# Both feature tiles of a pair in one run of gate matmuls: recurrent gates of a hybrid streaming block

## The chip, the cores and the metric

One core of a Trainium2 chip. TensorE (PE) multiplies, its weight loads (PEld) run beside it; VectorE (DVE), ScalarE (ACT) and GpSimd (POOL) do elementwise work; SyncE (SP) issues most of the transfers. The metric is the device time of one execution in microseconds, as the median of several. Less is better.

## The reference, cut to what matters

One layer over 512 frames of width 1024. The part that the change touches is the recurrent branch: a projection, a causal convolution, and two block-diagonal gates of 64x64 blocks that drive a linear recurrence.

```python
xn = rmsnorm(h, norm_mix_g[l])
u = jnp.einsum('bsd,de->bse', xn, w_in[l])
q, k, v, xr, gr, ga, gb = jnp.split(u, splits, axis=-1)
...
xc = causal_depthwise_conv(xr, conv_w[l], conv_b[l])
hr = rg_lru(xc, w_rg_r[l], b_rg_r[l], w_rg_i[l], b_rg_i[l], rg_lambda[l])
yb = (hr * jax.nn.gelu(gr)) @ w_rnn_out[l]

def rg_lru(x, w_r, b_r, w_i, b_i, lam):
    xb = x.reshape(B, S, N_RG_BLOCKS, RG_BLOCK)
    r = jax.nn.sigmoid(jnp.einsum('bsnd,nde->bsne', xb, w_r).reshape(B, S, D) + b_r)
    i = jax.nn.sigmoid(jnp.einsum('bsnd,nde->bsne', xb, w_i).reshape(B, S, D) + b_i)
    log_a = -RG_C * r * jax.nn.softplus(-lam)
    a = jnp.exp(log_a)
    bx = jnp.sqrt(-jnp.expm1(2.0 * log_a)) * (i * x)
    ...
```

## The kernel before

Features lie on the 128 partitions and frames on the free axis, so the 1024 features of a branch are eight tiles `j` of 128 x 512 (`S` is 512). All operands of TensorE are split into a high and a low part, and a product is three matmuls: high by high, high by low, low by high (`mm3`, lines 76 to 78). A projection of one tile, such as `po_xr`, is eight such triples, 24 matmuls of 512 columns.

The recurrent branch runs over pairs of tiles, `j` and `j + 1`, in the loop `for j in range(0, KT, 2)` at the end of the printed code: four pairs. For each pair come the two projections `po_xr` with their convolutions (`rnn_conv`), the two projections `po_gr` with their GeLU (`rnn_gelu`), the gates (`gates_of`, `rnn_gates`), and two projections `po_gb` for the merge gate (`gate`). In the first pair the `po_xr` and `po_gr` projections are done in two halves of 256 frames.

`rnn_conv` makes `xc` from `po_xr` with one activation (line 469) and three taps on VectorE (line 471). ScalarE copies it to the high part of `xch` (line 473), and POOL subtracts to get the low part (line 474). `rnn_gates` then multiplies `xch` with `wrg`, whose upper and lower 64 rows hold the blocks of one feature block each: six matmuls on half of the rows (line 492), alternating between the lower and the upper half (`e` is 1, then 0), each half into a bank of its own of the tile `rg`. Two matmuls on different halves of the rows can be in TensorE at the same time. Four activations of 64 partitions read the banks (lines 496 and 497), further ones and VectorE, POOL follow, and when both tiles of a pair have come so far, one square root over both (line 533) and the scans end it (`rnn_scan`). In `rnn_gelu`, the last VectorE step (line 483) is the last to read `po_gr`.

PSUM has eight banks here: four of the tag `mm`, in which most projections lie, two of the tag `t`, and the two of `rg`. A bank is written again when the engine that reads it last is through.

What sets the order: the program is written as above, and a scheduler places each instruction on its engine's queue by a simulated timeline, so the six matmuls of a run may come later than they are written. Inside the block `tc.manual_schedule` TensorE's instructions stay together in program order. Each queue is worked off in order; a waiting instruction holds what is behind it. POOL also computes the softplus of the recurrence's parameter (`sp_p`, lines 426 to 434) in many small steps, VectorE and ScalarE convert the weights (`whl`, lines 82 and 83), and VectorE forms differences of weight blocks that go back to memory (the spills, line 582).

Of the kernel before, what the change touches and what calls it, by code (L numbers as in the profile page):

```python
# [8 lines left out]
F32 = mybir.dt.float32  # L9
F32R = mybir.dt.float32r  # L10
AF = mybir.ActivationFunctionType
# [3 lines left out]
P = 128  # L15
D = 1024
S = 512
# [3 lines left out]
HD = 64  # L21
# [15 lines left out]
def block_kernel(ctx: ExitStack, tc: tile.TileContext, x, norm_mix_g, w_in, b_merge, rel_table,  # L37
# [3 lines left out]
    pe, dve, act, pool, sp = nc.tensor, nc.vector, nc.scalar, nc.gpsimd, nc.sync  # L41
# [23 lines left out]
    rgp = rg_stack.enter_context(tc.tile_pool(name="rg", bufs=1, space=PSUM, reuse_waits="tile"))  # L65
# [5 lines left out]
    def mm_tile(name, tag="mm"):  # L71
        return ps.tile([P, S], F32, tag=tag, bufs=4 if tag == "mm" else 2, name=name)
# [315 lines left out]
    hb = cp.tile([P, 40], F32, name="hb")  # L388
# [58 lines left out]
    wrg = rw2.tile([P, 2, 8, P], F32R, bufs=1, name="wrg")  # L447
# [8 lines left out]
    def halves(e):  # L456
        own, other = slice(e * HD, e * HD + HD), slice(HD - e * HD, 2 * HD - e * HD)
        return own, other
# [4 lines left out]
    def rnn_conv(j, po_xr):  # L463

        def tap(w):
            return vc[:, V_CW + 8 * w + j:V_CW + 8 * w + j + 1]

        xc = rw.tile([P, S], F32, tag="xc", name=f"xc{j}")
        act.activation(xc[:], po_xr[:], AF.Identity, bias=vc[:, V_CB + j:V_CB + j + 1], scale=tap(3))
        for d in range(1, 4):  # L470
            dve.scalar_tensor_tensor(xc[:, d:S], po_xr[:, 0:S - d], tap(3 - d), xc[:, d:S], ALU.mult, ALU.add)  # L471
        xch = rw2.tile([P, 2, S], F32R, tag="xch", name=f"xch{j}")
        act.activation(xch[:, 0], xc[:], AF.Copy)
        pool.tensor_sub(xch[:, 1], xc[:], f(xch[:, 0]))
        return xc, xch

    def rnn_gelu(j, po_gr):

        g = rw.tile([P, S], F32, tag="g", name=f"g{j}")
        act.activation(g[:], po_gr[:], AF.Square, scale=(GELU_C * GELU_A) ** 0.5)  # L480
        dve.scalar_tensor_tensor(g[:], g[:], GELU_C, po_gr[:], ALU.add, ALU.mult)
        act.activation(g[:], g[:], AF.Tanh)
        dve.scalar_tensor_tensor(g[:], g[:], 1.0, po_gr[:], ALU.add, ALU.mult)
        return g

    def rnn_gates(j, xc, xch, g):
        pos = rgp.tile([P, 2, S], F32, tag="rg", bufs=1, name=f"rg{j}")
        with tc.manual_schedule(engines={mybir.EngineType.PE}):
            for i, (w, x_) in enumerate(((0, 1), (0, 0), (1, 0))):
                for e in (1, 0):  # L490
                    rows = slice(e * HD, e * HD + HD)
                    pe.matmul(pos[:, e], wrg[rows, w, j], xch[rows, x_], start=i == 0, stop=i == 2)
        tr, ti = (rw.tile([P, S], F32, tag=f"gt{n}", bufs=(2, 3)[n], name=f"gt{j}_{n}") for n in range(2))
        for e in range(2):
            own, other = halves(e)
            act.activation(tr[own, :], pos[own, e], AF.Tanh, bias=hb[own, j:j + 1], scale=0.5)
            act.activation(ti[own, :], pos[other, e], AF.Tanh, bias=hb[other, 32 + j:33 + j], scale=0.5)
        if j % 2 == 0:
            u_pairs.append(rw.tile([P, 2, S], F32, tag="u", bufs=2, name=f"u{j}"))
        u = u_pairs[-1][:, j % 2]  # L500
        act.activation(u, tr[:], AF.Tanh, bias=sp2[:, j:j + 1], scale=sp2[:, j:j + 1])
        act.activation(tr[:], tr[:], AF.Exp, bias=spm4[:, j:j + 1], scale=spm4[:, j:j + 1])

        dve.scalar_tensor_tensor(u, tr[:], 1.0, u, ALU.add, ALU.mult)
        a = rw.tile([P, S], F32, tag="a", bufs=3, name=f"a{j}")
        pool.tensor_scalar(a[:], u, -1.0, 1.0, ALU.mult, ALU.add)

        dve.scalar_tensor_tensor(u, u, 2.0, u, ALU.subtract, ALU.mult)
        dve.scalar_tensor_tensor(ti[:], ti[:], 1.0, xc[:], ALU.add, ALU.mult)
        return j, u, a, ti, g  # L510
# [4 lines left out]
    def rnn_scan(j, u, a, ti, g):  # L515
        dve.scalar_tensor_tensor(ti[:], ti[:], 0.5, u, ALU.mult, ALU.mult)
        dve.tensor_tensor_scan(u, a[:], ti[:], 0.0, ALU.mult, ALU.add)
        dve.scalar_tensor_tensor(u, u, 0.5, g[:], ALU.mult, ALU.mult)
        if j % 2 == 0:
            rnn_pairs.append(big(j // 2, [P, 2, 2, S], F32R, f"rnn{j}"))  # L520
        o = rnn_pairs[-1][:, j % 2]
        act.activation(o[:, 0], u, AF.Copy)
        pool.tensor_sub(o[:, 1], u, f(o[:, 0]))
        return o
# [2 lines left out]
    rnn_pairs = []  # L527
    held = []

    def gates_of(j):  # L530
        held.append(rnn_gates(j, *conv.pop(j)))
        if len(held) == 2:
            act.activation(u_pairs[-1][:], u_pairs[-1][:], AF.Sqrt, scale=-1.0)
            while held:
                rnn.append(rnn_scan(*held.pop(0)))

    def tile_of(name, c, tag="mm", ahead=1):

        whl = weights(name, ahead)
        if (name, c) in first:  # L540
            po = first[name, c]
            project(po, whl, c, xnT, 256, S)
        else:
            po = mm_tile(f"po_{name}_{c}", tag)
            project(po, whl, c, xnT)
        return po
# [5 lines left out]
    def gate(w, j):  # L552
        po = tile_of(f"g{'ab'[w]}{j - j % 2}", j % 2)
        act.activation((ta, zB)[w][j], po[:], AF.Tanh, bias=hb[:, 16 + 8 * w + j:17 + 8 * w + j], scale=0.5)
# [37 lines left out]
    def spill_of(w, u, pl, tag, bufs):  # L592
        name, unit, to = {id(w_v): ("v", units_v, sums_v), id(w_o): ("o", units_o, sums_o)}.get(id(w), ("f", units, sums_d))
        r = [pl.tile([P, 2, S], F32, tag=tag, bufs=bufs, name=f"spill{name}{u}_{n}")[:] for n in range(4)]
        return spill(w, unit[u], to[u], r, w is w_o)
# [21 lines left out]
    def at_once(steps):  # L617
        for _ in steps:
            pass
# [3 lines left out]
    conv = {}  # L623
    for j in range(0, KT, 2):
        if j >= 4:
            at_once(spill_of(w_v, j // 2 - 2, early, "spill", 4))
        for c in range(2):
            conv[j + c] = rnn_conv(j + c, tile_of(f"xr{j}", c, ahead=2))
        for c in range(2):
            po = tile_of(f"gr{j}", c, "mm" if j == 0 else "t")  # L630
            conv[j + c] += (rnn_gelu(j + c, po),)
            gates_of(j + c)
        for c in range(2):
            gate(1, j + c)

# [714 lines left out]
    for j in range(4, FT, 2):  # L1350
# [5 lines left out]
        g, u = (sc.tile([P, 4, 256], F32, tag=f"c{w}", name=f"c_{w}{j}") for w in "gu")  # L1356
# [142 lines left out]
    with tc.manual_schedule(engines={mybir.EngineType.PE, mybir.EngineType.DVE, mybir.EngineType.Activation}):  # L1499
# [44 lines left out]
        x, w = acts["a22", last[0]], parts_w["t4", last[0]]  # L1544
# [39 lines left out]
```

## Time and profile before

| | |
|---|---|
| median of 3 runs | 852.59 us (852.57 to 852.69) |
| the profiled execution's own time | 852.42 us |
| its span | 850.5 us |
| mean granted clock of TensorE | 0.998 |
| matmuls of the gates, line 492 | 48, in 8 runs of six, from 43.3 to 145.9 us |
| activations on their banks, lines 496 and 497 | 32 of 64x512, about 0.68 us each |

The profile is of one execution, taken on the chip. A row of the timeline gives the start and the duration in us, the engine, the line in the program, the operation, what it writes and reads, the shape, and in brackets how long the engine sat idle before it and who released it. Matmuls are pipelined, so their rows overlap: the step from one start to the next is what one costs, not the duration. Rows of stretches give the busy time of each engine, then the granted clock of TensorE as a share of full speed (PEclk), then the transfers.

### The profile page before, as it was taken

The numbers are of one execution on the slowest core, as the hardware profiler recorded it, in microseconds if no ns is written. First come the engines' busy times: TensorE is split into PE (matmuls) and PEld (weight loads), VectorE is DVE, ScalarE is ACT, GpSimd is POOL, SyncE is SP. The second block draws the span as 40 slices with busy tenths as digits, with TensorE's granted clock in tenths as the row PEclk, the third lists the DMA queues.
The fourth block names the chain that finished last, engine by engine and source line by source line (L and its number), as shares of the span: only waits on it lengthen the run. The fifth ranks groups of instructions, "written<-read, shape, count | busy, mean of one in ns | idle before, by whom it ended". The sixth has DMA issues, their size and how long they took to land.

```text
span 850.5 us, 13164 instructions
## 1 busy us (share of the span) xinstructions
PE 839.3 (99%) x4836; PEld 733.8 (86%) x4836; DVE 676.0 (79%) x1029; ACT 513.8 (60%) x878; POOL 173.3 (20%) x192
## 2 busy tenths in 40 slices
PE   8999999999999999999999999999999999999997
PEld 6977887888888888888888889999999999988885
DVE  5789767699686777665678888998999897699985
ACT  7678686723665677656564558566465565285554
POOL 2324302220022576755500040000000001000002
PEclk9999999999999999999999999999999999999999
DMA  8684332695557246645456441677547332896622
GB/s 276 190 311 168 99 99 62 204 334 193 173 161 218 79 140 221 198 137 161 149 179 241 149 149 50 198 274 257 189 159 245 117 125 91 275 320 205 198 74 100
DMA packets 117776, 152.48 MB, mean 179 GB/s; under 512 B 7632, under 2 KB 86080, under 8 KB 117712
## 3 DMA queue, kind: packets, MB, share of 16 engines
q1 hardware_dynamic: 114032, 143.98, 52.0%
q10 hardware_dynamic: 3680, 7.67, 2.9%
q8 instruction: 38, 0.62, 0.3%
q14 instruction: 26, 0.21, 0.1%
HBM read 126.42 MB, written 25.21 MB: 178 GB/s over the span
## 4 chain that ended last, share of the span: by engine, by line
PE 90%; DVE 3%; POOL 3%; ACT 2%; issue 1%; DMA 1%; ACTq 0%; SPq 0%; DVEq 0%; POOLq 0%
PE po_out L76 4%; PE po_out L77 4%; PE po_out L78 4%; PE p_fu L76 3%; PE p_fu L77 2%; PE p_fu L78 2%; PE p_fg L76 2%; PE p_fg L77 2%; PE p_fg L78 2%; POOL p L718 2%; PE po_gb L76 2%; PE po_gb L77 2%; PE po_ya L78 2%; PE po_gb L78 2%; PE po_k L76 2%; PE po_ya L76 2%
## 5 line engine op out<-in xcount | busy, mean ns | idle before, releaser
L718 POOL TENSOR_SCALAR p<-p,rl 128x128 f32<-128x128 f32 (+1 forms) x64 | 49.3, 790 | 122.3 <-DVE rl L716 122.2
L1298 POOL TENSOR_TENSOR act_lo<-act,act_hi 128x1024 fp32r<-128x1024 f32 x1 | 2.4, 2422 | 215.9 <-ACT act_hi L1297 215.9
L713 ACT ACTIVATE p<-p,m 128x128 f32<-128x128 f32 (+1 forms) x64 | 35.7, 560 | 9.7 <-DVE m L712 9.5
L83 DVE TENSOR_TENSOR pp<-pT,pp 128x384 fp32r<-128x384 f32 (+1 forms) x48 | 28.6, 599 | 16.2 <-ACT pp L82 15.9
L83 DVE TENSOR_TENSOR whl_t<-raw_t,whl_t 128x1024 fp32r<-128x1024 f32 x26 | 31.6, 1214 | 0.3 <-ACT whl_t L82 0.3
L712 DVE CUSTOM_DVE_ANT_0 p<-s,bias 128x128 f32<-128x128 f32 (+1 forms) x64 | 29.5, 483 | 0.2
L1495 POOL TENSOR_TENSOR h<-h,g_fin 128x512 f32<-128x512 f32 x4 | 5.1, 1292 | 116.6 <-ACT oj L1491 116.6
L76 PE MATMUL po_gr<-xnT,whl_gr 128*128 128x512 f32 (+1 forms) x80 | 28.2, 354 | 0.1
L82 ACT ACTIVATE whl_t<-raw_t 128x1024 fp32r<-128x1024 f32 x26 | 27.2, 1046 | 1.5 <-PE po_h L78 1.5
L77 PE MATMUL po_xr<-xnT,whl_xr 128*128 128x512 f32 (+1 forms) x80 | 27.8, 353 | 0.0
L77 PE MATMUL po_gr<-xnT,whl_gr 128*128 128x512 f32 (+1 forms) x80 | 27.6, 347 | 0.0
L78 PE MATMUL po_gr<-xnT,whl_gr 128*128 128x512 f32 (+1 forms) x80 | 27.5, 348 | 0.0
L78 PE MATMUL po_xr<-xnT,whl_xr 128*128 128x512 f32 (+1 forms) x80 | 27.3, 346 | 0.0
L76 PE MATMUL po_xr<-xnT,whl_xr 128*128 128x512 f32 (+1 forms) x80 | 26.7, 352 | 0.6 <-ACT xnT L329 0.6
L76 PE MATMUL po_ga<-xnT,whl_ga 128*128 128x512 f32 x64 | 25.3, 396 | 0.3 <-DVE oacc L753 0.3
L83 DVE TENSOR_TENSOR whl_fg_s<-s_fg,whl_fg_s 128x1024 fp32r<-128x1024 f32 x18 | 21.9, 1220 | 4.7 <-ACT whl_fg_s L82 4.7
L76 PE MATMUL po_gb<-xnT,whl_gb 128*128 128x512 f32 x64 | 25.3, 395 | 0.2 <-DVE xc L471 0.2
L77 PE MATMUL po_gb<-xnT,whl_gb 128*128 128x512 f32 x64 | 25.2, 393 | 0.0
L76 PE MATMUL po_q<-xnT,whl_qk 128*128 128x512 f32 x64 | 25.1, 393 | 0.0
L78 PE MATMUL po_ga<-xnT,whl_ga 128*128 128x512 f32 x64 | 25.0, 390 | 0.0
L78 PE MATMUL po_q<-xnT,whl_qk 128*128 128x512 f32 x64 | 25.0, 390 | 0.0
L78 PE MATMUL po_ya<-aT,whl_ya 128*128 128x512 f32 x64 | 25.0, 390 | 0.0
(523 smaller groups left out, 3340.6 us busy)
## 6 DMA issues: line engine op xcount, KB each, us to landing
raw_t<-sums SPq DMA_DIRECT2D x20, 512.0 KB, 4.4
raw_fu<-in_w_ffn_in_dram SPq DMA_DIRECT2D x18, 512.0 KB, 4.1
raw_fg<-in_w_ffn_in_dram SPq DMA_DIRECT2D x18, 512.0 KB, 3.8
raw_qk<-in_w_in_dram SPq DMA_DIRECT2D x32, 256.0 KB, 3.5
raw_b<-in_w_ffn_out_dram SPq DMA_DIRECT2D x15, 512.0 KB, 4.8
spillf<-in_w_ffn_out_dram SPq DMA_DIRECT2D x12, 512.0 KB, 6.7
sums<-spillf SPq DMA_DIRECT2D x12, 512.0 KB, 3.0
raw_xr<-in_w_in_dram SPq DMA_DIRECT2D x8, 512.0 KB, 4.7
```

The costliest lines, as they stand in the source:

```text
L76: pe.matmul(o, sh, mh, start=start, stop=False, skip_group_check=parts)
L77: pe.matmul(o, sh, ml, start=False, stop=False, skip_group_check=parts)
L78: pe.matmul(o, sl, mh, start=False, stop=stop, skip_group_check=parts)
L82: act.activation(hi, src, AF.Copy)
L83: dve.tensor_sub(lo, src, f(hi))
L712: dve.tensor_tensor_reduce(prob[qb][:], scs[qb], bias[:, S - w:S], -1.0, 3e38, ALU.add, ALU.min, nmax[:, qb:qb + 1])
L713: exp = act.activation(prob[qb][:], prob[qb][:], AF.Exp, bias=nmax[:, qb:qb + 1], scale=-1.0, accum_out=lsum[:, qb:qb + 1])
L718: pool.tensor_scalar(prob[qb][:], prob[qb][:], rl[:, qb:qb + 1], 1.0, ALU.mult, ALU.mult)
L1298: pool.tensor_sub(lo[:], o[:], f(hi[:]))
L1495: eng.tensor_mul(hs, hs, g_fin[:, cc * S + at.start:cc * S + at.stop])
```

## The change

The matmuls leave `rnn_gates`, and a new function `rnn_products` does those of both tiles of a pair in one manually ordered block of twelve, after both GeLUs are written. The even tile keeps the two banks of `rg`; the odd tile takes two `mm` banks. The activations read the bank that they are given. Arithmetic, operands and the number of instructions on TensorE stay.

```diff
-    def rnn_gates(j, xc, xch, g):
-        pos = rgp.tile([P, 2, S], F32, tag="rg", bufs=1, name=f"rg{j}")
+    def rnn_products(js):
+        banks = {}
+        for j in js:
+            if j % 2:
+                banks[j] = [mm_tile(f"rg{j}_{e}")[:] for e in range(2)]
+            else:
+                both = rgp.tile([P, 2, S], F32, tag="rg", bufs=1, name=f"rg{j}")
+                banks[j] = [both[:, e] for e in range(2)]
         with tc.manual_schedule(engines={mybir.EngineType.PE}):
-            for i, (w, x_) in enumerate(((0, 1), (0, 0), (1, 0))):
-                for e in (1, 0):
-                    rows = slice(e * HD, e * HD + HD)
-                    pe.matmul(pos[:, e], wrg[rows, w, j], xch[rows, x_], start=i == 0, stop=i == 2)
+            for j in js:
+                for i, (w, x_) in enumerate(((0, 1), (0, 0), (1, 0))):
+                    for e in (1, 0):
+                        rows = slice(e * HD, e * HD + HD)
+                        pe.matmul(banks[j][e], wrg[rows, w, j], conv[j][1][rows, x_], start=i == 0, stop=i == 2)
+        return banks
+
+    def rnn_gates(j, pos, xc, xch, g):
         tr, ti = (rw.tile([P, S], F32, tag=f"gt{n}", bufs=(2, 3)[n], name=f"gt{j}_{n}") for n in range(2))
         for e in range(2):
             own, other = halves(e)
-            act.activation(tr[own, :], pos[own, e], AF.Tanh, bias=hb[own, j:j + 1], scale=0.5)
-            act.activation(ti[own, :], pos[other, e], AF.Tanh, bias=hb[other, 32 + j:33 + j], scale=0.5)
+            act.activation(tr[own, :], pos[e][own], AF.Tanh, bias=hb[own, j:j + 1], scale=0.5)
+            act.activation(ti[own, :], pos[e][other], AF.Tanh, bias=hb[other, 32 + j:33 + j], scale=0.5)
...
-    def gates_of(j):
-        held.append(rnn_gates(j, *conv.pop(j)))
+    def gates_of(j, pos):
+        held.append(rnn_gates(j, pos, *conv.pop(j)))
...
             conv[j + c] += (rnn_gelu(j + c, po),)
-            gates_of(j + c)
+        banks = rnn_products((j, j + 1))
+        for c in range(2):
+            gates_of(j + c, banks[j + c])
```

The scheduler answers with another order. TensorE in the first pair before, from the end of the second `po_gr` (`po_gr0_1`) on; `po_gb0_0` goes on for 24 matmuls:

```order
L76 MATMUL po_gr0_1_356<-xnT_158,whl_gr0_4_328 128x256
L77 MATMUL po_gr0_1_356<-xnT_158,whl_gr0_4_328 128x256
L78 MATMUL po_gr0_1_356<-xnT_158,whl_gr0_4_328 128x256
L76 MATMUL po_gb0_0_690<-xnT_158,whl_gb0_0_491 128x512 [waits DVE_49,Activation_49]
L77 MATMUL po_gb0_0_690<-xnT_158,whl_gb0_0_491 128x512
```

and at the end of `po_gb0_0`, where tile 0's run of six (`rg0`, on `xch0`) stood:

```order
L77 MATMUL po_gb0_0_690<-xnT_158,whl_gb0_4_496 128x512
L78 MATMUL po_gb0_0_690<-xnT_158,whl_gb0_4_496 128x512
L492 MATMUL rg0_592<-xch0_528,wrg_431 128x512 [waits Pool_49]
L492 MATMUL rg0_592<-xch0_528,wrg_431 128x512
L492 MATMUL rg0_592<-xch0_528,wrg_431 128x512 [waits Activation_49]
L492 MATMUL rg0_592<-xch0_528,wrg_431 128x512 x3
L76 MATMUL po_gb0_1_716<-xnT_158,whl_gb0_0_491 128x512 [waits Activation_49]
```

Tile 1's run followed 15 matmuls into the next pair's first `po_xr`. TensorE at the same place with the change (`rg1_0` and `rg1_1` are the odd tile's two `mm` banks):

```order
L78 MATMUL po_gr0_1_356<-xnT_158,whl_gr0_4_328 128x256
L499 MATMUL rg0_621<-xch0_528,wrg_431 128x512 [waits Pool_49]
L499 MATMUL rg0_621<-xch0_528,wrg_431 128x512
L499 MATMUL rg0_621<-xch0_528,wrg_431 128x512 [waits Activation_49]
L499 MATMUL rg0_621<-xch0_528,wrg_431 128x512 x3
L499 MATMUL rg1_1_623<-xch1_560,wrg_431 128x512 [waits PE_49,Pool_49]
L499 MATMUL rg1_0_622<-xch1_560,wrg_431 128x512 [waits DVE_49,PE_49]
L499 MATMUL rg1_1_623<-xch1_560,wrg_431 128x512 [waits Activation_49]
L499 MATMUL rg1_0_622<-xch1_560,wrg_431 128x512
L499 MATMUL rg1_1_623<-xch1_560,wrg_431 128x512
L499 MATMUL rg1_0_622<-xch1_560,wrg_431 128x512
L76 MATMUL po_gb0_0_688<-xnT_158,whl_gb0_0_491 128x512 [waits DVE_49]
```

All twelve have moved ahead of both `po_gb`, and the run waits for POOL twice, for `xch0` and for `xch1`. In the three later pairs the twelve stand in the same way between the second `po_gr` and the first `po_gb`; before, a pair's first run stood in the middle of the second `po_gr` or just ahead of it, and its second run within a `po_gb`.

ScalarE around the first pair's gates before (`xch1` is tile 1's high part, `zb0` the activation on `po_gb`):

```order
L482 ACTIVATE g0_587<-g0_587 128x512 [waits DVE_49]
L482 ACTIVATE g1_640<-g1_640 128x512 [waits DVE_49]
L554 ACTIVATE zb0_438<-po_gb0_0_690,hb_385 128x512 [waits PE_49]
L496 ACTIVATE gt0_0_602<-rg0_592,hb_385 64x512 [waits PE_49]
L497 ACTIVATE gt0_1_603<-rg0_592,hb_385 64x512
L496 ACTIVATE gt0_0_602<-rg0_592,hb_385 64x512
L497 ACTIVATE gt0_1_603<-rg0_592,hb_385 64x512
L473 ACTIVATE xch1_560<-xc1_555 128x512 [waits DVE_49,Activation_49]
```

and with the change:

```order
L482 ACTIVATE g0_587<-g0_587 128x512 [waits DVE_49]
L506 ACTIVATE gt0_0_639<-rg0_621,hb_385 64x512 [waits PE_49]
L507 ACTIVATE gt0_1_640<-rg0_621,hb_385 64x512
L506 ACTIVATE gt0_0_639<-rg0_621,hb_385 64x512
L507 ACTIVATE gt0_1_640<-rg0_621,hb_385 64x512
L482 ACTIVATE g1_616<-g1_616 128x512 [waits DVE_49]
L473 ACTIVATE xch1_560<-xc1_555 128x512 [waits DVE_49,Activation_49]
```

The second GeLU step `g1` has gone behind tile 0's four gate activations, `zb0` further back; `xch1` still stands behind tile 0's gates.

## The prediction

> **What bounds the kernel now.** I read the busy times first, then the chain that ended last, then TensorE's waits.
>
> ```profile
> PE 839.3 (99%) x4836; PEld 733.8 (86%) x4836; DVE 676.0 (79%) x1029; ACT 513.8 (60%) x878; POOL 173.3 (20%) x192
> PE 90%; DVE 3%; POOL 3%; ACT 2%; issue 1%; DMA 1%; ACTq 0%; SPq 0%; DVEq 0%; POOLq 0%
> PE pT L731 <- POOL p L718: 1.3, 4, 0.3
> PE busy L278 <- DVE eps_t L284: 1.2, 1, 1.2
> L492 PE MATMUL rg<-xch,wrg x48: 386/394/497, 43.3 to 145.9; 64*128 64x512 f32 x48
> ```
>
> TensorE is busy for 99% of the span and carries 90% of the chain. In the list of waits (total us, times, longest) its longest single wait is 1.2 us, at the start. So there is no idle time later on in which a new stall could be absorbed: a microsecond that TensorE loses early is a microsecond at the end. The question is then what the change does to TensorE's own time in the four feature pairs, and whether the longer run must wait for its operands. The gate matmuls run from 43.3 to 145.9 us, so all of it lies in the first sixth of the span.
>
> **What one run of six costs.** From the timeline of TensorE, second pair (start, duration, instruction):
>
> ```profile
> 69.73 0.39 PE L78 MATMUL po_gr<-xnT,whl_gr 128*128 128x512 f32 x1
> 70.05 0.50 PE L492 MATMUL rg<-xch,wrg 64*128 64x512 f32 x2
> 70.38 0.62 PE L492 MATMUL rg<-xch,wrg 64*128 64x512 f32 x4
> 70.62 0.39 PE L492 MATMUL rg<-xch,wrg 64*128 64x512 f32 x2
> 70.94 0.50 PE L76 MATMUL po_gr<-xnT,whl_gr 128*128 128x512 f32 x1
> 73.58 0.39 PE L78 MATMUL po_gr<-xnT,whl_gr 128*128 128x512 f32 x1
> 73.81 0.39 PE L76 MATMUL po_gb<-xnT,whl_gb 128*128 128x512 f32 x1
> ```
>
> Plain matmuls of 512 columns start 0.227 us apart (73.58 to 73.81). From 69.73 to 73.81 there are 13 of those steps, 2.95 us, so the run of six cost 4.08 - 2.95 = 1.13 us. The half-row matmuls go two at a time: pairs start at 70.05, 70.38 and 70.62, so a third pair behind a second costs 0.24 us. Three pairs more in the same run would cost 3 x 0.24 = 0.72 us, and a run of twelve saves 1.13 - 0.72 = **0.41 us** against two of six. The bounds: 0.45 if the added pairs go at the plain step of 0.227, 0.24 if six more cost all the 0.89 us that lie between 70.05 and 70.94.
>
> The ideal gain is therefore 4 x 0.41 = 1.6 us. No row tells this from no change safely: 0.2% of the time, 1.7 us, is about what a measurement can separate.
>
> **The wait that it adds.** In the changed order TensorE's queue holds the first pair's twelve matmuls right behind the second `po_gr` and ahead of both `po_gb`. The six of tile 0 wait for POOL's `xch0`, the six of tile 1 for POOL's `xch1`; behind them is everything else that TensorE does. When is each there? In the order of POOL, ScalarE and VectorE up to `xch1`, only two things differ: the four gate activations of tile 0 now stand ahead of the second `L482`, and `zb` of `po_gb` has gone behind.
>
> ```profile
> 37.19 0.28 PE L78 MATMUL po_gr<-xnT,whl_gr 128*128 128x256 f32 x1
> 37.66 0.47 PE L76 MATMUL po_gb<-xnT,whl_gb 128*128 128x512 f32 x1 [0.19 <-DVE xc L471]
> 43.30 0.96 PE L492 MATMUL rg<-xch,wrg 64*128 64x512 f32 x6
> 41.51 0.23 POOL L433 TENSOR_SCALAR sp_p<-sp_p 128x8 f32<-128x8 f32 x1
> 41.70 1.30 POOL L474 TENSOR_TENSOR xch<-xc,xch 128x512 fp32r<-128x512 f32 x1
> 47.83 1.95 POOL L474 TENSOR_TENSOR xch<-xc,xch 128x512 fp32r<-128x512 f32 x1 [3.68 <-ACT xch L473]
> 46.00 0.74 DVE L471 SCALAR_TENSOR_TENSOR xc<-po_xr,vc,xc 128x509 f32<-128x509 f32 x1
> 44.30 0.68 ACT L496 ACTIVATE gt<-rg,hb 64x512 f32<-64x512 f32 x1 [0.21 <-PE rg L492]
> 47.12 0.63 ACT L473 ACTIVATE xch<-xc 128x512 fp32r<-128x512 f32 x1
> 47.65 0.80 ACT L501 ACTIVATE u<-gt,sp 128x512 f32<-128x512 f32 x1
> ```
>
> - TensorE is through with `po_gr` at 37.19 + 0.12 = 37.31. Before, it began `po_gb` at 37.66 and worked until 43.30.
> - `xch0` is ready at 41.70 + 1.30 = 43.00: it sits on POOL behind the small operations of the softplus (`sp_p`), whose order does not change. A released matmul started 0.15 us after its releaser (`xc` 37.51, `po_gb` 37.66), so the first six start at 43.15. **Idle: 43.15 - 37.31 = 5.8 us.**
> - The gate activations started 1.00 us after the run (43.30, 44.30) and the four took 2.82 us until 47.12. Now: 44.15 to 46.97. Then the second `L482`, about 0.53 us (the step from 47.12 to 47.65 for the same shape), then `xch1` on ScalarE at 47.50. `xc1` is ready at 46.74, so VectorE is not last. The step to POOL's start was 0.71 us (47.12, 47.83): 48.21. I take the same instruction's 1.95 us, since VectorE works beside it as before: ready at 50.16, second six at 50.31.
> - The first six end at 43.15 + 0.89 = 44.04. **Idle: 50.31 - 44.04 = 6.3 us.**
>
> The sum of the first pair: 5.8 + 6.3 of new idle time, less the 0.35 us that TensorE waited before `po_gb` (37.31 to 37.66), less what the idle hides of two runs' entries and exits: each run's 1.13 is 0.68 of streaming and 0.45 of the rest, of which only the last exit, about 0.35, is still paid, so 0.55. That is **+11.2 us**. With POOL's subtraction at 1.30 it is 10.6, at its longest, 3.25, it is 12.5.
>
> ```profile
> L474 POOL TENSOR_TENSOR xch<-xc,xch x8: 1285/1296/3245, 41.7 to 138.9; 128x512 fp32r<-128x512 f32 x8
> 76.42 3.25 POOL L474 TENSOR_TENSOR xch<-xc,xch 128x512 fp32r<-128x512 f32 x1 [10.75 <-issue]
> 104.99 1.28 POOL L474 TENSOR_TENSOR xch<-xc,xch 128x512 fp32r<-128x512 f32 x1 [0.68 <-POOL xch L474]
> 138.86 1.29 POOL L474 TENSOR_TENSOR xch<-xc,xch 128x512 fp32r<-128x512 f32 x1 [4.17 <-issue]
> 108.71 0.39 PE L76 MATMUL po_gb<-xnT,whl_gb 128*128 128x512 f32 x1
> 138.03 0.50 PE L76 MATMUL po_gr<-xnT,whl_gr 128*128 128x512 f32 x1
> ```
>
> The other three pairs: a run now stands behind the whole second `po_gr` instead of inside it or later, so its odd tile is wanted earlier. In the third pair `xch5` is ready at 106.27 (104.99 + 1.28) and that place is at 108.71 - 1.13 = 107.6; in the fourth `xch7` is ready at 140.15 and the place at 138.03 + 24 x 0.227 - 1.13 = 142.4. In the second `xch3` was ready at 79.67 only, and 73.81 - 1.13 = 72.7 would have been the place. But before, VectorE put the first pair's scans between the taps of `xc3`; now these are done while TensorE stands still, and the taps follow `po_xr` directly. I count `xch3` ready some 6 us after its `po_xr`, with the place 10.9 us after it (two `po_gr`). So I expect no wait in these, and a gain of 3 x 0.41 = **-1.2 us** (-0.7 to -1.35).
>
> **The clock.** Two pauses of about 6 us with 0.9 us of work between them are longer than any that TensorE has had. Its granted clock (the column PEclk of the stretches) shows what a pause does, at the end of this trace, and its first matmuls show what a restart costs:
>
> ```profile
> 843.89 0.28 PE L78 MATMUL po_rest<-whl_t,x_a 128*128 128x256 f32 x1
> 845.00:846.00 1.00, 0.00 (x0) 0.00 (x0) 0.87 (x5) 0.55 (x3) 0.00 (x0) 1.00 0.00 0
> 846.00:847.00 1.00, 0.00 (x0) 0.00 (x0) 0.58 (x2) 0.61 (x1) 0.00 (x0) 0.86 0.00 0
> 847.00:848.00 1.00, 0.00 (x0) 0.00 (x0) 0.00 (x0) 0.00 (x0) 0.00 (x0) 0.50 0.45 181
> L278 PE MATMUL busy<-idle x16: 379/634/634, 1.2 to 7.3; 128*128 128x512 bf16 x16
> ```
>
> The last matmul starts at 843.89 and the clock stands at 0.50 from about 846.72 (0.28 of that microsecond at half gives its 0.86): 2.7 us of idle time were enough. At the start, 16 matmuls of 512 columns start between 1.18 and 7.3, 0.41 us apart, where 0.227 is the later step: 15 x 0.18 = 2.7 us lost until full speed. I take that as the price of the restart at the second six (another number type, so an estimate; 0 if the clock holds, 3.4 if the slow stretch lasts a microsecond or two longer). The first six run slow too: 0.7 us more (three steps of 0.24 doubled; 0 to 0.9), which delays the gates and with them `xch1`. Together **+3.4 us**.
>
> [...]
>
> **Edits that cost nothing here.** The odd tile's gates take two of the four `mm` banks, and `po_gb` of the first pair now waits for VectorE to leave `po_gr`'s bank: `L483` did that by 45 us, TensorE comes at 51. ScalarE loads one activation table more:
>
> ```profile
> 44.27 0.68 DVE L483 SCALAR_TENSOR_TENSOR g<-g,po_gr 128x512 f32<-128x512 f32 x1
> 64.26 1.28 ACT L533 ACT_TABLE_LOAD   x1
> 51.38 1.22 DVE L83 TENSOR_TENSOR whl_gr<-raw_gr,whl_gr 128x1024 fp32r<-128x1024 f32 x1
> ```
>
> Its 1.28 us lie beside the 11 us of both `po_gb`; without that cover they would delay the next pair's weights by as much. Those are the edit to watch: `whl_gr` of the second pair, 51.38 before, now stands on VectorE behind the whole first pair up to the scans. Counted on from the gates at 51.3: eight gate and decay operations to 55.6, table and root to 59.3, scans, products and two of the spill's subtractions to about 67, the conversion to 68.2. TensorE needs it after `po_gb` and `po_xr`, 4 x 5.45 us from 51.2: 73. Five us to spare. On SP the loads of `raw_gb` and `raw_xr` have gone behind more of the spill's stores; they are for use after 84 us.
>
> **The sum.** The profiled execution took 852.42 us (span 850.5), 0.17 under the median of the three runs, 852.59. 852.42 + 11.2 - 1.2 + 3.4 = **865.8 us**.
>
> **The rivals.**
> - *The clock holds* through the pauses, or falls too late to matter: 865.8 - 3.4 = 862.4. For it: the pauses are cut by six matmuls. Against it: the drop after 2.7 us. Chance 0.12.
> - *A second stall follows*: the first pair's work on VectorE and ScalarE is bunched, and if a spill's load comes late, the second pair's `whl_gr` misses the 73 us, or its `xch3` the end of `po_gr` at 84. Both have about 5 us to spare; a slip of 8 gives 865.8 + 3 = 868.8. Chance 0.07.
> - *Not slower*: both `xch` are there when TensorE arrives. Then only the merging counts, 852.42 - 4 x 0.41 = 850.8. It would need `xch1` before 37.3; but `xc1` alone leaves VectorE at 46.74, and nothing ahead of it there has moved. That the twelve do not run as one is ruled out by the order. Chance 0.03, of which 0.01 lies within 0.2%.
>
> **The numbers.** The forecast, with the stall and the clock, has 0.78, and by its terms' bounds goes from about 863.5 to 868. The range takes in the clock's rival: 862.0 to 868.5. Faster by over 0.2%: 0.02; within: 0.01; slower: 0.97.
>
> **What would show it.** Right: TensorE idle for some 6 us before the first `rg` matmul and again before the seventh, both times with POOL's `xch` as the releaser; `po_gb` beginning at 51 to 53 us instead of 37.66; a granted clock of 0.50 there; later runs of twelve taking about 1.85 us with no wait ahead. Wrong: no pause between the sixth and seventh matmul, a pause at a later pair, or a clock of 1.00 from 37 to 60 us.

## The result and the profile after

The changed kernel takes **864.58 us** (median of 4 runs, 863.81 to 865.69); the kernel before took 852.64 us beside it (852.57 to 853.10). The ratio is 1.0141, 95% interval 1.0129 to 1.0154: slower, as forecast, by 1.2 us less than the forecast of 865.8. The profiled execution is the fastest of the four, 863.81 us.

The page of the changed kernel, its rows on the span, the busy times, the granted clock and the chain:

```profile
span 861.9 us, 13162 instructions
PE 839.6 (97%) x4836; PEld 735.8 (85%) x4836; DVE 680.7 (79%) x1029; ACT 514.8 (60%) x878; POOL 173.3 (20%) x192
PEclk9979999999999999999999999999999999999999
PE 87%; POOL 4%; DVE 3%; ACT 2%; DMA 1%; issue 1%; ACTq 0%; SPq 0%; DVEq 0%; POOLq 0%
```

TensorE works for as long as before (839.6 against 839.3 us), in a span that is 11.4 us longer, so what was added is idle time. The third slice of the clock (43 to 65 us) reads 7 tenths, where it read 9 before, and POOL's share of the chain went from 3% to 4%. The list of TensorE's waits (total us, times, longest) has one new row of more than 1 us, and the timeline shows where it lies and what the clock does to the matmuls behind it:

```profile
PE rg L499 <- POOL xch L474: 10.9, 2, 5.6
```
```profile
37.15 0.28 PE L78 MATMUL po_gr<-xnT,whl_gr 128*128 128x256 f32 x1
42.98 1.65 PE L499 MATMUL rg<-xch,wrg 64*128 64x512 f32 x6 [5.55 <-POOL xch L474]
50.03 1.72 PE L499 MATMUL rg<-xch,wrg 64*128 64x512 f32 x6 [5.39 <-POOL xch L474]
51.68 0.80 PE L76 MATMUL po_gb<-xnT,whl_gb 128*128 128x512 f32 x1
52.27 0.63 PE L77 MATMUL po_gb<-xnT,whl_gb 128*128 128x512 f32 x1
...
53.55 0.47 PE L77 MATMUL po_gb<-xnT,whl_gb 128*128 128x512 f32 x1
53.86 0.39 PE L78 MATMUL po_gb<-xnT,whl_gb 128*128 128x512 f32 x1
54.09 0.39 PE L76 MATMUL po_gb<-xnT,whl_gb 128*128 128x512 f32 x1
```

Two pauses stand where the forecast put them, before the first gate matmul and before the seventh, and `po_gb` begins at 51.68 instead of 37.66 us. Up to 53.55 the matmuls go at half speed (0.43 us from start to start), then at the usual 0.23. The stretches of the same trace (the number before the last two is the granted clock) give the moments: it falls at 40.06 and is back at 53.72.

```profile
40.00:41.00 1.00, 0.00 (x0) 0.00 (x0) 1.00 (x2) 0.15 (x1) 0.99 (x1) 0.53 0.19 54
42.00:50.00 8.00, 1.65 (x6) 0.84 (x6) 7.23 (x11) 5.22 (x8) 3.34 (x3) 0.50 0.66 238
53.00:54.00 1.00, 1.00 (x4) 0.77 (x4) 0.69 (x1) 0.95 (x3) 0.28 (x1) 0.64 0.90 195
```

The later pairs do run as one, without a wait ahead. The second pair in the timeline:

```profile
85.17 0.39 PE L78 MATMUL po_gr<-xnT,whl_gr 128*128 128x512 f32 x1
85.48 1.66 PE L499 MATMUL rg<-xch,wrg 64*128 64x512 f32 x12
87.07 0.50 PE L76 MATMUL po_gb<-xnT,whl_gb 128*128 128x512 f32 x1
```

From the last matmul ahead to the first behind are 1.90 us, where a run of six took 1.21 before (69.73 to 70.94). Six more cost 0.69 us instead of 1.13.

The account closes in this execution. `po_gb` starts 14.02 us late and its first matmuls lose another 0.9 us to the clock (51.68 to 54.09 are 2.41 us, for 0.34 + 5 x 0.23 = 1.49). Off go the two runs of six that stood later before, 2.26, and three merges of 0.44: 14.02 + 0.92 - 2.26 - 1.3 = 11.4 us, as measured (863.81 against 852.42).

### The profile page after: what moved, and what is told of

Same layout as the page of the kernel before. It is cut to its first block, busy times and chain, and to the rows that moved or that the text cites. A ratio compares the mean times of both kernels' runs of the same rounds, so it can differ in the third digit from the quotient of the medians.

```text
span 861.9 us, 13162 instructions
## 1 busy us (share of the span) xinstructions
PE 839.6 (97%) x4836; PEld 735.8 (85%) x4836; DVE 680.7 (79%) x1029; ACT 514.8 (60%) x878; POOL 173.3 (20%) x192
## 4 chain that ended last, share of the span: by engine, by line
PE 87%; POOL 4%; DVE 3%; ACT 2%; DMA 1%; issue 1%; ACTq 0%; SPq 0%; DVEq 0%; POOLq 0%
PE po_out L76 4%; PE po_out L77 4%; PE po_out L78 4%; PE p_fu L76 2%; PE p_fu L77 2%; PE p_fu L78 2%; PE p_fg L76 2%; PE p_fg L77 2%; PE p_fg L78 2%; POOL p L730 2%; PE po_gb L76 2%; PE po_gb L77 2%; PE po_gb L78 2%; PE po_ya L76 2%; PE po_ya L77 2%; PE po_ya L78 2%
## 5 line engine op out<-in xcount | busy, mean ns | idle before, releaser
L730 POOL TENSOR_SCALAR p<-p,rl 128x128 f32<-128x128 f32 (+1 forms) x64 | 47.5, 762 | 122.1 <-DVE rl L728 122.0
L76 PE MATMUL po_gb<-xnT,whl_gb 128*128 128x512 f32 x64 | 25.9, 405 | 0.0
L77 PE MATMUL po_gb<-xnT,whl_gb 128*128 128x512 f32 x64 | 25.3, 395 | 0.0
L83 DVE TENSOR_TENSOR whl_qk<-raw_qk,whl_qk 128x1024 fp32r<-128x1024 f32 x16 | 20.9, 1327 | 5.3 <-ACT whl_qk L82 5.1
L78 PE MATMUL po_gb<-xnT,whl_gb 128*128 128x512 f32 x64 | 25.1, 393 | 0.0
L76 PE MATMUL po_q<-xnT,whl_qk 128*128 128x512 f32 x64 | 25.1, 393 | 0.0
```

Source lines behind the costliest of these rows:

```text
L76: pe.matmul(o, sh, mh, start=start, stop=False, skip_group_check=parts)
L77: pe.matmul(o, sh, ml, start=False, stop=False, skip_group_check=parts)
L78: pe.matmul(o, sl, mh, start=False, stop=stop, skip_group_check=parts)
L83: dve.tensor_sub(lo, src, f(hi))
L730: pool.tensor_scalar(prob[qb][:], prob[qb][:], rl[:, qb:qb + 1], 1.0, ALU.mult, ALU.mult)
```

## The experiments

Three things were open. Why does the run stand ahead of both `po_gb` at all: because it is one run of twelve, or because of the banks? Does the merging as such save what the rows say, in a pair that does not stall? And what do the two parts of the loss, the pauses and the clock, cost each by itself?

| kernel | median us | ratio to before, on the same chip | 95% interval |
|---|---|---|---|
| the change | 864.58 | 1.0141 | 1.0129 to 1.0154 |
| e4_banks_alone | 865.98 | 1.0150 | 1.0137 to 1.0164 |
| e1_first_apart | 860.19 | 1.0083 | 1.0069 to 1.0097 |
| e2_behind_gb | 866.59 | 1.0161 | 1.0147 to 1.0175 |
| e3_kept_busy | 866.87 | 1.0159 | 1.0145 to 1.0173 |
| e3b_busy_longer | 865.22 | 1.0140 | 1.0127 to 1.0154 |
| e8_busy_low_on_dve | 862.97 | 1.0114 | 1.0097 to 1.0131 |
| e5_first_only | 865.49 | 1.0144 | 1.0130 to 1.0158 |
| e7_last_two | 852.06 | 0.9988 | 0.9979 to 0.9997 |

### The banks without the run of twelve

The kernel before, with its eight separate runs of six, but the odd tile in two `mm` banks:

```diff
-            gates_of(j + c)
+            gates_of(j + c, rnn_products((j + c,))[j + c])
```

> Runs of six for each tile again, written where they were before, with the odd tile in two mm banks: the banks without the run of twelve. If the banks decide (the odd tile takes the two banks that are free first, so both po_gb are left with banks that the second convolution and the second GeLU hold until 46 and 47 us): pauses ahead of both runs of the first pair as in the changed kernel, about 864.6 + 3 x 0.2 to 3 x 0.42 = 865.2 to 865.9 us. If the run of twelve decides: no pauses and 852.6 us.

Measured: ratio 1.0150, and the changed kernel's row among the waits:

```profile
PE rg L499 <- POOL xch L474: 11.0, 2, 5.6
```

So the banks alone bring the whole stall. In the built program the first pair's `po_xr` and `po_gr` hold all four `mm` banks. Before, `po_gb` took the bank of `po_xr0`, which the taps of `xc0` free at about 37.5 us. Now the odd tile takes that bank and the one of `po_gr0`, and `po_gb` is left with the banks of `po_xr1` and `po_gr1`, still to be read by the second convolution (its last tap ends at 46.66 us) and the second GeLU. For the scheduler `po_gb` is then the later of the two, and the gates go first. The place of the run is therefore not the harm by itself: put first, `po_gb` would have waited for the bank of `po_xr1` until about 46.7 us (an estimate from that last tap). What a run of twelve in other banks would do was not run.

### The first pair as before, three pairs merged

```diff
-            if j % 2:
+            if j % 2 and j > 1:
...
+            if j == 0:
+                gates_of(c, rnn_products((c,))[c])
-        banks = rnn_products((j, j + 1))
-        for c in range(2):
-            gates_of(j + c, banks[j + c])
+        if j:
+            banks = rnn_products((j, j + 1))
+            for c in range(2):
+                gates_of(j + c, banks[j + c])
```

> The change undone in the first pair alone: its two tiles have a run of six each in the banks of rg, as before; the three later pairs keep the run of twelve with the odd tile in mm banks. My theory (the whole loss comes from the first pair, and a run of twelve saves about 0.42 us against two of six): 852.6 - 3 x 0.42 = 851.3 us, no wait ahead of any gate matmul, clock 1.00 throughout the pairs. Rival, that a longer run saves nothing (the time between runs is only moved): 852.6 us. Rival, that the later pairs lose too by the banks they take: above 853 us.

Measured: ratio 1.0083, where 851.3 us would have been 0.9985. A clear miss, by more than 8 us: the stall has moved into the second pair. The waits and the timelines of TensorE and POOL there:

```profile
PE rg L499 <- POOL xch L474: 7.2, 2, 6.2
```
```profile
73.92 0.39 PE L78 MATMUL po_gr<-xnT,whl_gr 128*128 128x512 f32 x1
74.24 0.96 PE L499 MATMUL rg<-xch,wrg 64*128 64x512 f32 x6
81.38 1.65 PE L499 MATMUL rg<-xch,wrg 64*128 64x512 f32 x6 [6.18 <-POOL xch L474]
77.58 3.74 POOL L474 TENSOR_TENSOR xch<-xc,xch 128x512 fp32r<-128x512 f32 x1 [9.62 <-issue]
```

This is the place that the prediction weighed: `xch3` was ready only at 79.67 us before, and the run wants it at 72.7. Here it is ready at 81.32, wanted at 75.1. In the changed kernel nothing waits there, because VectorE and POOL catch up while TensorE stands in the first pair: VectorE's first scan (`u<-a,gt`) begins there at 63.56 us, before the second pair's `po_xr` are through (74.5), and here at 73.75, 10 us after them (63.3). The first stall hides the second. So merging is free in the second pair only after a stall has been paid for. There is a smaller miss as well: the other wait of the row, 1.1 us, is that of the first pair's second run at 54.75 us, since POOL's subtraction for `xch1` took 6.52 us. The two waits, the second pair's second six at half speed (0.7) and the slow start of `po_gb` (0.8), less three merges (1.3), are 7.4 us. In the profiled execution the first `po_q`, the product behind the four pairs, begins 8.0 us later than before (163.67 against 155.63), 0.4 of it from ahead of the gates (`po_gb` began at 38.02 instead of 37.66).

### The products written behind both `po_gb`

```diff
+        for c in range(2):
+            gate(1, j + c)
         banks = rnn_products((j, j + 1))
         for c in range(2):
             gates_of(j + c, banks[j + c])
-        for c in range(2):
-            gate(1, j + c)
```

> The products written behind both po_gb of their pair, so that po_gb takes its banks first. In the order the first pair then has tile 0's six between the po_gb and tile 1's six behind them; the later pairs have twelve behind the second po_gb. If the first pair's loss comes from the banks that the odd tile takes ahead of po_gb: no 5 us pauses there, po_gb begins near 37.7 us, and the merging gives 851.3 us, unless the last pair's scans, now some 10 us later, are late for po_yb; then up to 5 us more, seen as a wait of po_yb for rnn at about 165 us (851 to 857). If the loss came from having both tiles' products in one block: pauses of 5 us at 37 to 50 us and 863 us or more.

Measured: ratio 1.0161, another miss. `po_gb` takes its bank first and covers the wait for `xch0`, so the first pause is gone. But the seventh matmul still waits, 4.4 us, and a new wait of 4.2 us appears in a later stage. There TensorE waits for VectorE's `zb`, which stands at 200.58 us behind VectorE's other work, without a gap since 182.0; the wait for `rnn` that was expected there is only 0.4 us. The waits; POOL's subtraction that makes `xch1`; and VectorE's last instructions before it came to an end:

```profile
PE rg L499 <- POOL xch L474: 4.4, 1, 4.4
PE po_yb L76 <- DVE zb L894: 4.2, 1, 4.2
```
```profile
48.10 6.50 POOL L474 TENSOR_TENSOR xch<-xc,xch 128x512 fp32r<-128x512 f32 x1 [3.70 <-ACT xch L473]
...
51.65 0.69 DVE L514 SCALAR_TENSOR_TENSOR u<-gt,u 128x512 f32<-128x512 f32 x1
52.25 1.22 DVE L83 TENSOR_TENSOR whl_gr<-raw_gr,whl_gr 128x1024 fp32r<-128x1024 f32 x1
```

The subtraction of 128x512 took 1.27 us in the changed kernel and 6.50 here. It ends 1.13 us after VectorE's first gap (52.25 + 1.22 = 53.47, and 54.60). In this order VectorE's instructions follow each other without a gap from 47.64 to 53.47, and `xch1` is there at 54.60 instead of 49.98: the order that covers the first wait delays the second operand. In its twelve the scheduler put a whole `po_gb` between the first six and the second: the ordered block keeps only the order of its own instructions, and others may stand between. To that extent the description above, that they stay together, is too strong.

### TensorE kept busy in the pauses

Matmuls of 128x512 without a use go ahead of each six of the first pair, into a bank that the gates then overwrite:

```diff
+                for _ in range((24, 22)[j] if j < 2 else 0):
+                    pe.matmul(banks[j][0], xnT[0][:, 0, 0:P], xnT[0][:, 0], start=True, stop=True)
```

> The changed kernel with matmuls of no use in the first pair's two pauses: 24 ahead of the first six (into a bank that the first six then begin anew) and 22 ahead of the second six, 0.227 us each; results unchanged. They end before POOL's xch is there, so the waits stay and only the clock differs. My theory, that the pauses halve the clock and that this costs 0.7 us at the first six and 1.7 us from the second six on in the profiled execution: clock 1.00 from 36 to 60 us, activations on the first bank 1.0 us after its run begins instead of 1.69, po_gb from about 50.3 us, and 864.6 - 3 = 861.4 to 862 us, with its runs within 0.5 us of each other, since the moment at which the clock falls and returns no longer varies. Rival, that the clock has no part: 864.6 us and a spread of 1.9 us as now.

Measured: ratio 1.0159, a miss whose time decides nothing. POOL's subtraction for `xch1` took 4.47 us this time, so 22 matmuls were too few: TensorE paused for 2.9 us after all, and the clock fell at 51.38 and came back at 58.22. The waits and stretches:

```profile
PE rg L501 <- POOL xch L474: 2.9, 1, 2.9
```
```profile
51.00:52.00 1.00, 0.00 (x0) 0.00 (x0) 0.00 (x0) 0.00 (x0) 1.00 (x1) 0.69 0.96 166
58.00:59.00 1.00, 1.00 (x5) 0.78 (x5) 1.00 (x2) 0.32 (x1) 0.00 (x0) 0.89 0.03 12
```

The same with 36 matmuls in the second pause instead of 22:

> As e3_kept_busy, with 36 instead of 22 idle matmuls ahead of the second six, so that no pause of TensorE is longer than about 1 us: GpSimd's subtraction on xch1 ends at 52.1 there. Theory: the pauses stay, so the clock is the only difference. If half clock is a cost of its own, the granted clock reads 1.00 through 40 to 60 us and the time is e3's 866.9 less 3.1 (6.2 us at half speed in e3), 863.8. If the clock costs nothing beside the pauses, 866.9 again.

Measured: 865.22 us, ratio 1.0140. The granted clock now stays at 1.00 and no wait for `xch` is left in the list. Stretches, TensorE, POOL and VectorE:

```profile
48.00:52.00 4.00, 4.00 (x19) 3.34 (x18) 2.99 (x4) 1.25 (x2) 4.00 (x1) 1.00 0.72 217
52.00:56.00 4.00, 4.00 (x20) 2.77 (x20) 0.69 (x1) 2.57 (x4) 0.73 (x2) 1.00 0.92 287
```
```profile
52.37 0.96 PE L501 MATMUL rg<-xch,wrg 64*128 64x512 f32 x6
47.62 4.52 POOL L474 TENSOR_TENSOR xch<-xc,xch 128x512 fp32r<-128x512 f32 x1 [3.44 <-ACT xch L473]
47.43 1.22 DVE L594 TENSOR_TENSOR spillv<-spillv,spillv 128x1024 f32<-128x1024 f32 x1
48.57 0.68 DVE L521 SCALAR_TENSOR_TENSOR gt<-gt,xc 128x512 f32<-128x512 f32 x1
49.17 1.22 DVE L594 TENSOR_TENSOR spillv<-spillv,spillv 128x1024 f32<-128x1024 f32 x1
50.31 0.68 DVE L516 SCALAR_TENSOR_TENSOR u<-gt,u 128x512 f32<-128x512 f32 x1
```

It is 1.6 us faster than `e3_kept_busy` with a second six that starts 0.23 later. That is half of the 3.1 expected, and the intervals of the two ratios overlap; the profiled executions are 2.4 us apart (867.60 and 865.22), and the traces, compared below, show that half clock costs time of its own. The spread of the runs went from 1.9 us (865.73 to 867.60) to 0.15, but the kernel before, which has no pause, spread as much as 1.9 us too (852.33 to 854.20 beside `e3_kept_busy`). But the pause is longer here than in the changed kernel, by POOL's subtraction: VectorE's four instructions follow each other without a gap, POOL's is issued beside the first and ends 1.15 us after the last (50.99 and 52.14).

If VectorE's instructions are the reason, the subtraction should come earlier in VectorE's own queue:

```diff
-        pool.tensor_sub(xch[:, 1], xc[:], f(xch[:, 0]))
+        (dve if j < 2 else pool).tensor_sub(xch[:, 1], xc[:], f(xch[:, 0]))
...
-                for _ in range((24, 36)[j] if j < 2 else 0):
+                for _ in range((24, 25)[j] if j < 2 else 0):
```

> As e3b_busy_longer, but the first pair's two subtractions for the low part of xch (line 474) stand on VectorE instead of GpSimd, and 25 idle matmuls fill the second pause. Theory: on GpSimd the second one took 4.52 us in e3b only because VectorE's own subtractions (1.2 us each) went ahead of it; in VectorE's queue it stands behind one of them and one product and ends at about 49.9 instead of 52.1. The second six then start at about 50.0 instead of 52.37, the clock stays at 1.00, and the time is e3b's 865.2 less 2.4: 862.8, ratio 1.0112. If GpSimd's long duration is only a matter of how its span is recorded, xch1 was ready earlier all along and the time stays at 865.2.

Measured: 862.97 us, ratio 1.0114, on the expectation of 862.8 and 1.0112. So the long duration on GpSimd was a real wait, and not only a matter of its record. The subtraction takes 0.69 us, the second six start at 50.19, the clock stays:

```profile
49.36 0.69 DVE L474 TENSOR_TENSOR xch<-xc,xch 128x512 fp32r<-128x512 f32 x1
50.19 0.96 PE L501 MATMUL rg<-xch,wrg 64*128 64x512 f32 x6 [0.19 <-DVE xch L474]
```
```profile
44.00:52.00 8.00, 7.81 (x37) 5.95 (x36) 7.78 (x12) 5.82 (x10) 0.05 (x1) 1.00 0.73 248
52.00:60.00 8.00, 8.00 (x37) 6.63 (x36) 3.67 (x5) 5.52 (x7) 1.20 (x2) 1.00 0.87 296
```

This kernel is also the best measure of the clock. Its second six start at 50.19, those of the changed kernel at 50.03: the same pauses, one with full and one with half clock. The medians differ by 864.58 - 862.97 = 1.6 us, the ratios by 0.0027, 2.3 us, on different chips. The traces give it more closely. From the start of the second six to the first `po_xr` of the second pair, TensorE does the same in all of these kernels, six matmuls and two `po_gb` (`e5_first_only` follows below):

| kernel | second six start, us | half clock behind it until | first `po_xr` | from six to `po_xr` |
|---|---|---|---|---|
| e8_busy_low_on_dve | 50.19 | none | 62.09 | 11.90 |
| e3b_busy_longer | 52.37 | none | 64.29 | 11.92 |
| the change | 50.03 | 53.72 | 63.63 | 13.60 |
| e5_first_only | 49.84 | 55.80 | 64.50 | 14.66 |
| e3_kept_busy | 52.14 | 58.22 | 66.81 | 14.67 |

Behind the second pause the clock thus costs 1.7 us in the changed kernel and 2.8 in the two whose half speed lasts 6 us instead of 3.7.

### The merges alone

Only the first pair changed, the three later pairs as before (`if j == 1` for the banks, `if j == 0` for the common run):

> Only the first pair is changed (run of twelve, odd tile in two projection banks); the three later pairs are as before. If each later merge saves 0.42 us, as the rows of the changed kernel say (six more matmuls 0.69 us instead of 1.13), the time is the changed kernel's plus 1.26: 865.8, ratio 1.0155. If the merges save nothing, 864.6; if they lose something that the first pair's stall hides, below 864.

Measured: ratio 1.0144, where 1.0155 was expected with a gain in the later merges and 1.0141 would be without any. The interval holds both, so the medians leave it undecided. The traces decide it. From the second six to the first `po_q` are 119.38 us here (49.84 to 169.22) and 116.99 in the changed kernel (50.03 to 167.02), 2.39 more. Of these the clock, which came back later here (55.80), explains 14.66 - 13.60 = 1.06, by the table; the other 1.33 are 0.44 for each of three merges. The stretches with the clock's fall and return:

```profile
42.00:43.00 1.00, 0.20 (x2) 0.20 (x4) 1.00 (x2) 0.00 (x0) 1.00 (x2) 0.57 1.03 370
55.00:56.00 1.00, 1.00 (x4) 0.79 (x3) 0.05 (x1) 0.97 (x2) 0.00 (x0) 0.60 1.01 391
```

The other way round, only the last two pairs merged, the first two as before:

```diff
-            if j % 2:
+            if j % 2 and j > 3:
...
+            if j < 4:
+                gates_of(j + c, rnn_products((j + c,))[j + c])
-        banks = rnn_products((j, j + 1))
+        if j >= 4:
+            banks = rnn_products((j, j + 1))
```

> The first two pairs as before, the last two merged with the odd tile in two projection banks. Theory: no row of the kernel before or of e1 shows the last two pairs' run waiting, so each merge is its 0.42 us and the time is before less 0.84: ratio 0.9990. Rival: in the third pair the odd tile's xch is late without the first pair's stall, as the second pair's was in e1: 5 to 8 us more, ratio 1.006 to 1.009.

Measured: ratio 0.9988, 0.9979 to 0.9997, with 0.9990 expected. Here the interval leaves out 1, and no wait on `xch` appears. In the profiled executions the first `po_q` begins at 154.77 us, against 155.63 before: 0.86 us, two merges of 0.43. The third pair in the timeline:

```profile
107.41 0.39 PE L78 MATMUL po_gr<-xnT,whl_gr 128*128 128x512 f32 x1
107.73 1.65 PE L499 MATMUL rg<-xch,wrg 64*128 64x512 f32 x12
109.31 0.50 PE L76 MATMUL po_gb<-xnT,whl_gb 128*128 128x512 f32 x1
```

From 107.41 to 109.31 are the 1.90 us of the changed kernel. This is the version that beats both, by 0.12%: the edit is sound where its operands are ready, and the gain is as small as the rows of before said.

## Why the prediction was right, and where its sizes were off

**That nothing later absorbs a stall: right.** TensorE's busy time did not change, and the account above needs no recovery further on.

**One run of six, and the merge: right.** 0.69 us for six more instead of 1.13 is a gain of 0.44, forecast 0.41; `e7_last_two` and the traces of `e5_first_only` show it in the time.

**The first pause: right**, 42.98 - 37.27 = 5.7 us against 5.8; `xch0` was on POOL at 41.67 to 42.93.

**The second pause: right in its mechanism, 1.0 us too long.** By the prediction's steps, with the slow first six, the second would have started at 51.0; it started at 50.03. The chain went as worked out:

```profile
44.67 0.68 ACT L506 ACTIVATE gt<-rg,hb 64x512 f32<-64x512 f32 x1 [4.52 <-PE rg L499]
...
48.02 0.61 ACT L473 ACTIVATE xch<-xc 128x512 fp32r<-128x512 f32 x1
48.71 1.27 POOL L474 TENSOR_TENSOR xch<-xc,xch 128x512 fp32r<-128x512 f32 x1 [4.64 <-ACT xch L473]
48.75 2.31 DVE L592 TENSOR_TENSOR spillv<-spillv,spillv 128x1024 f32<-128x1024 f32 x1
```

The step that failed was "I take the same instruction's 1.95 us, since VectorE works beside it as before". POOL began 0.04 us ahead of VectorE's subtraction, took 1.27 us, and it was VectorE's that stretched, from 1.22 to 2.31. The bound of 1.30 that the prediction kept was the right value. This is 0.7 of the 1.0 us; the rest is small steps of the chain.

**The clock: right that it falls in the first pause and stays down through the second, 1.0 us too dear.** The term "15 x 0.18 = 2.7 us lost until full speed" was mis-sized: the second six lost 0.76 (51.68 - 50.03, less the 0.89 of full speed) and `po_gb` 0.92, together 1.7 us, since the clock came back 3.7 us after the restart. The term took its 6 us from the kernel's first 16 matmuls, 0.41 us apart until 7.3; the clock column reads 1.00 there in the trace of before, so that these were slow by the clock was the author's estimate. But 1.7 is the value of this execution: in `e5_first_only`, with the same two pauses, the clock came back after 6.0 us and cost 2.76, the size that was forecast. So the traces show both sizes behind the same two pauses. The first six lost the 0.7 forecast (the gates start 1.69 us after the run instead of 1.00). These two terms make the difference in the profiled run: 865.8 - 1.0 - 1.0 = 863.8. The median lies 0.8 above it, within the spread of the runs.

**The second pair: right, with half of the margin counted.** The scans were done before the taps of `xc3`, as the prediction said, and without the first stall `xch3` is 6.2 us late, as `e1_first_apart` shows. But it was there at 82.88, 8.4 us after its `po_xr` (74.5) and not about 6: VectorE converted two blocks of `whl_gb` (74.90 to 78.49) ahead of its taps. That left 2.6 us before the run at 85.48, where 4.9 were counted. `whl_gr` came at 70.49 (its first half) for a use at 74.51: 4 us to spare, where 5 were counted.

**What the prediction did not ask** is why the run moved ahead of `po_gb`. It took the order as given, which was enough for the time, and put the two `mm` banks under the edits that cost nothing. `e4_banks_alone` shows that they alone move the run and bring the stall, without the run of twelve. The prediction also took `po_gb`'s bank to be free by 45 us; its readers were through at 46.66 (the taps of `xc1`), which made no difference, as TensorE came at 51.68. Without the experiment, one would have looked for the cure in the wrong place, as `e2_behind_gb` did.

## What to carry to other kernels

Before a product is given spare PSUM banks, look up who would have had them next: here two banks for a gain of 0.4 us a pair took away the work that had covered an 11 us wait. Merging short runs moves the later one's operands forward, so compare, pair by pair, when its last operand is ready with where the merged run will stand, and merge only where it is early; and do not trust a pair that is early only because another one stalled. When TensorE must pause for several microseconds (the clock fell in pauses of 2.9 us in `e3_kept_busy` and 5.6 in the changed kernel), count the half-speed stretch behind the pause as well, here 1.7 to 2.8 us.

## What the runs showed of the hardware that was not expected

**The clock changed at moments that lie multiples of 3.41 us apart.** In the changed kernel it fell at 40.06 and returned at 53.72, 13.66 us later, four times 3.41. In `e5_first_only` it was 42.14 and 55.80, again 13.66; in `e3_kept_busy` 51.38 and 58.22, 6.84, two times 3.42; in `e4_banks_alone` 39.60 and 56.66, 17.06, five times 3.41. `e2_behind_gb` paused twice, at 50 and at about 200 us. Its stretches:

```profile
53.00:54.00 1.00, 0.00 (x0) 0.00 (x0) 0.48 (x1) 0.00 (x0) 1.00 (x1) 0.96 0.79 205
60.00:61.00 1.00, 1.00 (x5) 0.76 (x4) 0.13 (x1) 0.82 (x1) 0.00 (x0) 0.62 1.13 410
200.00:202.00 2.00, 0.67 (x2) 0.58 (x3) 1.97 (x4) 0.00 (x0) 0.00 (x0) 0.68 1.04 422
```

It fell at 53.92, returned at 60.76 and fell again at 200.72, 146.80 us after the first time: 43 times 3.414. The step of 3.41 us is worked out from these moments: 17.06 - 13.66 = 3.40, and 13.66 - 6.84 = 6.82 is twice that. Counted in such steps, the one at whose end the clock fell was not wholly idle: it still had work in its first 0.6 us in the changed kernel (until about 37.3, of 36.65 to 40.06) and in its first 1.3 us in `e3_kept_busy`; and steps with work from 49.84 on (48.97 to 52.38 in `e5_first_only`) and from 50.25 on (49.83 to 53.24 in `e4_banks_alone`) did not bring it back, while one worked through (50.30 to 53.72 in the changed kernel) did. In these runs half speed lasted 3.7 us where the restart came 0.27 us ahead of a step (the changed kernel), 6.0 to 6.4 us where it came 0.4 to 0.9 us into one (`e5_first_only`, `e3_kept_busy`, `e4_banks_alone`), and 3.3 us where it came 0.15 us into one (`e1_first_apart`: fall at 77.82, restart at 81.38, return at 84.66). That the place of the restart in such a step is what spreads the times of one kernel is not shown: the kernel before, without a pause, spread by up to 1.9 us as well, and in `e3_kept_busy` the execution of 865.73 us had a mean clock of 0.996, that of 867.07 one of 0.997.

**Some instructions of VectorE and GpSimd took longer beside each other.** The same subtraction on GpSimd took 1.27 us (changed kernel), 1.95 (before), 3.74 (`e1_first_apart`, second pair), 4.52 (`e3b_busy_longer`) and 6.50 (`e2_behind_gb`). In the two longest of these it ended 1.1 to 1.2 us after VectorE's first pause. In `e1_first_apart` VectorE went on with line 481, which reads `po_gr` in PSUM, and the subtraction ended at 81.32, 1.12 us after the VectorE instruction ahead of that (line 83, to 80.20). In the other direction, VectorE's subtraction beside GpSimd's took 2.31 us in the changed kernel instead of 1.22. In `e3b_busy_longer` four VectorE instructions in a row, begun at 47.43 to 50.31 us, kept their usual 1.22 and 0.68 us while GpSimd's lasted. In the kernel before, GpSimd's began at 47.83 beside one VectorE subtraction that kept its 1.22 us (47.40), and the next of VectorE's (line 509, 48.53 us) took 1.79 us instead of 0.69. Why, and which of the two goes first, no run shows.
